# Block A's attention values as one 128-column stationary operand in a two-layer hybrid attention encoder

## The chip, the cores and the metric

One core of one Trainium2 chip runs the whole program in one launch. The metric is the device time of that launch in microseconds (us), the median over the runs shown; lower is better. The kernel before takes 1463.04 us (three runs, 1462.65 to 1463.38).

## The reference, cut to what matters

Two layers, each with three kinds of attention (A, B, C) on a sequence of 1024 and a width of 1024. The change is in the weighted sum of the values of A, the dilated attention of four heads of 64 features:

```python
DILATED_PATTERNS = ((128, 1), (512, 4), (2048, 16))
def dilated_attention(q, k, v, slopes):
    for window, dil in DILATED_PATTERNS:
        ...
        p = jnp.exp(s - m)
        den = jnp.sum(p, axis=-1, keepdims=True)
        o = jnp.einsum('bndhij,bnjdhe->bnidhe', (p / den).astype(v.dtype), vw)
        lse = (m + jnp.log(den))[..., 0]
        ...
    w = jax.nn.softmax(jnp.stack(lses, axis=0), axis=0)
    out = jnp.sum(w[..., None] * jnp.stack(outs, axis=0), axis=0)

    # in each layer
    ya = dilated_attention(qa, ka, va, slopes).reshape(B, S, A_WIDTH) * jax.nn.silu(ag)
    yb = dense_attention(qb, kb, vb) * jax.nn.silu(bg)
    yc = dense_attention(qc, kc, vc) * jax.nn.silu(cg)
    y = jnp.concatenate([ya, yb, yc], axis=-1)
    x = x + y @ w_out[l]
```

## The kernel before

Float32 products are made on TensorE from pairs: each operand is split into a high part (rounded to the type that TensorE takes in one pass) and a low part (the rest), and high x high, high x low and low x high are added up in PSUM. Values lie in scratch memory as 128 columns per head: 64 high, 64 low (`v_evac`), so that a tile of values can be loaded with both parts side by side.

A layer first makes the projections and the gates, and then runs the attention of 16 heads in an order that is planned by hand: `put(slot, step, priority)` files every step of every head under a slot of a common counter, and `slot` (L1219) emits the steps of one slot by priority. ScalarE (`A`) executes them in that order; on the other engines (`T` TensorE, `V` VectorE, `G` GpSimd) and in SyncE's queue of DMAs the scheduler of the language orders what has been emitted, by its own estimate of when operands are ready and by the order of emission. B's six heads come first, then A's four (slots `base_a + 4` to `base_a + 36` and some), then C's six; the scores of C's first head are made while A's last heads are worked on. Between A's steps stand partial output projections, `f_load`, `f_mm` and `f_add` (L1093 to L1124), of features that are already there. `f_load` fetches a piece of the output weights and a strip of x, has GpSimd split the weights, and is filed `FL` slots ahead of its products (L1190).

A head of A goes through these steps:
- `a_s` (L897 to L913): scores of the window pattern and of the "class" pattern (the two dilated ones, by residue of the position), bias and maximum by VectorE; `a_exp` (L920, L922): exponentials by ScalarE.
- The statistics chain, `a_x1` to `a_x5` (L926 to L986): small VectorE steps on columns of maxima and sums (L929, L944 to L951, L962 to L969, L983, L986), with two products by TensorE (L937, L977) that move values between partitions, and one exponential (L956). Out come the weights of the two patterns.
- `a_norm_w` (L992) and `a_norm_c` (L996): GpSimd multiplies the probabilities by those weights, eight tiles each.
- `a_t` (L1009, L1014, L1015, L1019, L1020): TensorE transposes them, and `split_pt` (L782, L783) splits them into high (`ph`) and low (`pl`) on ScalarE and VectorE.
- `a_v` (L1029 to L1068): the products with the values, in three passes with 64 stationary columns each: `w[:, LO]` with `ph`, `w[:, LO]` with `pl`, `w[:, HI]` with `ph` (L1038 to L1040 for the class, L1051 to L1053 for the window). All three add to the same 64 PSUM partitions.
- `a_end` (L1077): ScalarE copies the class result into `y` (L1085), VectorE adds the window result to it (L1088). After the second head of a pair GpSimd multiplies by the gate (`fin_gate`, L820), and ScalarE and GpSimd split the product (`fin_split`, L836, L837).

The heads of B and C already use 128 stationary columns and two passes (`tv_v`, L801 and L802), with the halves added in `tv_end` (L839 to L854).

PSUM tiles of 512 columns for transposes and for accumulators come from the same four buffers. `H` (L67) is a pool of six SBUF buffers of 512 columns that holds, among others, the split output weights of `f_load` and the copies `t0` and `t1` of `tv_end`.

Of the kernel before, what the change touches and what calls it, by code (L numbers as in the profile page):

```python
# [11 lines left out]
AF = mybir.ActivationFunctionType  # L12
ALU = mybir.AluOpType
AX = mybir.AxisListType

P = 128
# [21 lines left out]
def hybrid_encoder(  # L38
# [8 lines left out]
    V, G, A, T = nc.vector, nc.gpsimd, nc.scalar, nc.tensor  # L47

    cp = ctx.enter_context(tc.tile_pool(name="consts", bufs=1))
    sp = ctx.enter_context(tc.tile_pool(name="work", bufs=1))  # L50
# [6 lines left out]
    def nm(s):  # L57
        uid[0] += 1
        return f"{s}_{uid[0]}"
# [5 lines left out]
        return sp.tile(list(shape), dt, tag="QB", name=nm("qb"), bufs=8)  # L65

    def H(dt=F32, shape=(P, 512)):  # L67
        return sp.tile(list(shape), dt, tag="H", name=nm("h"), bufs=6)

    def WR(dt=F32, shape=(P, 512)):  # L70
        return sp.tile(list(shape), dt, tag="Wr", name=nm("wr"), bufs=3)
# [203 lines left out]
    def layer(l, xh, xl, ss, g, bg_x):  # L275
# [14 lines left out]
        for k in range(8):  # L290
# [12 lines left out]
            for m, half in order:  # L303
                w = slice(m * P, m * P + P)
                o = bk[m][half]
                s = slice(half * 512, half * 512 + 512)
# [90 lines left out]
        for k in range(8):  # L397
            w = ws.next(3)
# [4 lines left out]
            if k == SK:  # L403
                lat_stats()
                r, r2, fq, fkv = lat_factors()
# [30 lines left out]
        for c in range(NCH):  # L436
            s = slice(c * P, (c + 1) * P)
            pq = PS()
            for half in range(2):
                o = pq[:, half * 512:half * 512 + 288]  # L440
                w = slice(half * 288, half * 288 + 288)
# [6 lines left out]
        for c in range(NCH):  # L448
            s = slice(c * P, (c + 1) * P)
# [262 lines left out]
        LO, HI = slice(0, 64), slice(64, 128)  # L712
# [65 lines left out]
        accs, PTs = {}, {}  # L778
# [250 lines left out]
        def a_v(h, i):  # L1029
            ph, pl = PTs.pop(("a", h, i))  # L1030
            if i < 4:
                if i % 2 == 0:
                    accs["a", h, "c"] = PA()
                o = accs["a", h, "c"][LO, (i % 2) * 256:(i % 2) * 256 + 256]
                for kb in range(2):
                    w = Vcl[h][:, 2 * i + kb, :]
                    s = slice(kb * 256, kb * 256 + 256)
                    T.matmul(o, w[:, LO], ph[:, s], start=(kb == 0), stop=False)  # L1038
                    T.matmul(o, w[:, LO], pl[:, s], start=False, stop=False)
                    T.matmul(o, w[:, HI], ph[:, s], start=False, stop=(kb == 1))  # L1040
                if i % 2 == 1:
                    a_end(h, "c", i // 2)
                return
            if i == 4:
                accs["a", h, 0] = PA()
            if i == 5:
                accs["a", h, 1] = PA()

            def mm(half, q0, w, rows, cols, start=False, stop=False):
                o = accs["a", h, half][LO, q0 * P:q0 * P + (cols.stop - cols.start)]  # L1050
                T.matmul(o, w[rows, LO], ph[rows, cols], start=start, stop=False, skip_group_check=True)  # L1051
                T.matmul(o, w[rows, LO], pl[rows, cols], start=False, stop=False, skip_group_check=True)
                T.matmul(o, w[rows, HI], ph[rows, cols], start=False, stop=stop, skip_group_check=True)  # L1053

            full = slice(0, P)
            if i == 4:
                mm(0, 0, Vs[h][:, 1, :], full, slice(0, 256), start=True)
                mm(0, 1, Vs[h][:, 2, :], full, slice(256, 512))
            elif i == 5:
                mm(0, 2, Vs[h][:, 3, :], full, slice(0, 256))  # L1060
                mm(0, 3, Vs[h][:, 4, :], full, slice(256, 384))
                mm(1, 0, Vs[h][:, 4, :], full, slice(384, 512), start=True)
            elif i == 6:
                mm(1, 0, Vs[h][:, 5, :], full, slice(0, 256))
                mm(1, 1, Vs[h][:, 6, :], full, slice(256, 512))
            else:
                mm(0, 0, Vs[h][:, 0, :], LO, slice(256, 384), stop=True)
                mm(1, 2, Vs[h][:, 7, :], full, slice(0, 256))  # L1068
                mm(1, 3, Vs[h][:, 8, :], LO, slice(384, 512), stop=True)
                a_end(h, 0, 0)  # L1070
                a_end(h, 1, 1)
                for n in range(4):
                    Pa.pop((h, n))
# [3 lines left out]
        def a_end(h, what, half):  # L1077
            acc = accs.pop(("a", h, what))
            fc, par = feat(("a", h))
            if fc not in pairs:  # L1080
                gate_load(fc)
            rows = slice(64 * par, 64 * par + 64)
            y = pairs[fc][0]
            if what == "c":
                A.activation(y[rows, half * 512:half * 512 + 512], acc[LO], AF.Copy)  # L1085
            else:
                yv = y.rearrange("p (r s i) -> p s r i", r=4, s=2)[rows, half]
                V.tensor_tensor(yv, acc[LO].rearrange("p (i r) -> p r i", r=4), yv, ALU.add)  # L1088


        Fw, Fx, Fp = {}, {}, {}
# [43 lines left out]
        start = {hd: 16 * i + (8 * AH + AT0 if hd[0] == "c" else 0) for i, hd in enumerate(heads)}  # L1135
# [6 lines left out]
        for i, hd in enumerate(heads):  # L1142
            for c in range(NCH):
                s = start[hd] + 2 * c - LAG_D
# [36 lines left out]
        for h in range(AH):  # L1181
# [4 lines left out]
            if h % 2:  # L1186
                for half in range(2):
                    put(base_a + AT0 + 8 * h + FA[0] + half, lambda h=h, half=half: fin_gate(h // 2, half), 6)
                    put(base_a + AT0 + 8 * h + FA[1] + half, lambda h=h, half=half: fin_split(h // 2, half), 6)
        F0, FN, FP, FL = -10, 5, 6.5, 8  # L1190
        for i, m in enumerate(EARLY):
            s = base_a + F0 + FN * i
            put(s - FL, lambda m=m: f_load(m), 9)
# [5 lines left out]
        for i, hd in enumerate(heads):  # L1199
            kind, h = hd  # L1200
# [259 lines left out]
```

## Time and profile before

| | before |
|---|---|
| median of 3 runs | 1463.04 us |
| profiled execution | 1461.05 us |
| its span | 1459.1 us |
| instructions | 23134 |
| TensorE busy | 1443.1 us (99%) |
| VectorE busy | 1094.5 us (75%) |
| ScalarE busy | 899.4 us (62%) |
| GpSimd busy | 574.3 us (39%) |
| granted TensorE clock | 1.00 |

The span runs from the first to the last instruction of the profiled execution; the 1.95 us more of its own time lie around it. PE is TensorE's products, PEld its weight loads, DVE VectorE, ACT ScalarE, POOL GpSimd, SPq SyncE's DMA queue. Products are pipelined, so the busy time of one in the trace is longer than its share of the engine; the share is read from start to start.

### The profile page before, as it was taken

The numbers are of one execution on the slowest core, as the hardware profiler recorded it, in microseconds if no ns is written. First come the engines' busy times: TensorE is split into PE (matmuls) and PEld (weight loads), VectorE is DVE, ScalarE is ACT, GpSimd is POOL, SyncE is SP. The second block draws the span as 40 slices with busy tenths as digits, with TensorE's granted clock in tenths as the row PEclk, the third lists the DMA queues.
The fourth block names the chain that finished last, engine by engine and source line by source line (L and its number), as shares of the span: only waits on it lengthen the run. The fifth ranks groups of instructions, "written<-read, shape, count | busy, mean of one in ns | idle before, by whom it ended". The sixth has DMA issues, their size and how long they took to land.

```text
span 1459.1 us, 23134 instructions
## 1 busy us (share of the span) xinstructions
PE 1443.1 (99%) x7912; PEld 1227.4 (84%) x7912; DVE 1094.5 (75%) x1997; ACT 899.4 (62%) x1678; POOL 574.3 (39%) x516
## 2 busy tenths in 40 slices
PE   9999999999999999999999999999999999999999
PEld 7998888888888888888889988888888888888887
DVE  7759767488888789994736597574888787899942
ACT  6473234488888769993425723343888886799820
POOL 6204431135455565550322054211454554754500
PEclk9999999999999999999999999999999999999999
DMA  6261136610287821102622611465103688121143
GB/s 223 80 245 59 52 107 207 207 44 30 51 202 204 243 84 51 44 26 75 212 81 90 238 40 47 166 198 156 59 30 76 172 242 235 31 59 30 44 148 121
DMA packets 118134, 171.81 MB, mean 118 GB/s; under 512 B 11520, under 2 KB 73088, under 8 KB 118016
## 3 DMA queue, kind: packets, MB, share of 16 engines
q1 hardware_dynamic: 118016, 170.32, 38.2%
q8 instruction: 63, 1.03, 0.3%
q14 instruction: 55, 0.45, 0.1%
HBM read 109.47 MB, written 60.82 MB: 117 GB/s over the span
## 4 chain that ended last, share of the span: by engine, by line
PE 90%; DVE 4%; ACT 3%; DMA 1%; issue 1%; SPq 0%; POOL 0%; ACTq 0%; DVEq 0%
PE S L760 15%; PE T L789 11%; PE acc L802 6%; PE acc L801 6%; PE T L669 4%; PE T L667 4%; PE T L668 4%; PE S L1262 3%; PE S L1260 3%; PE S L1261 3%; PE S L221 2%; PE S L222 2%; PE S L223 2%; PE T L705 1%; PE T L221 1%
## 5 line engine op out<-in xcount | busy, mean ns | idle before, releaser
L783 DVE TENSOR_TENSOR wl<-T,wh 128x512 fp32r<-128x512 f32 x440 | 297.0, 685 | 69.2 <-ACT wh L782 67.2
L782 ACT ACTIVATE wh<-T 128x512 fp32r<-128x512 f32 x440 | 261.2, 596 | 115.7 <-PE T L789 77.4
L776 POOL TENSOR_SCALAR u<-u,rec 128x1024 f32<-128x1024 f32 x192 | 216.5, 1128 | 277.4 <-DVE rec L775 176.7
L760 PE MATMUL S<-u,u 96*128 96x512 f32 (+1 forms) x960 | 268.7, 409 | 0.5 <-ACT u L769 0.3
L762 DVE TENSOR_REDUCE nmax<-S 128x1 f32<-128x1024 f32 x192 | 233.7, 1217 | 23.7 <-PE S L760 23.2
L789 PEld LDWEIGHTS T<-ident,u 128*128 128x128 f32 x1536 | 190.8, 140 | 49.0 <-DVE wl L783 0.4
L789 PE MATMUL T<-ident,u 128*128 128x128 f32 x1536 | 230.0, 272 | 0.0
L769 ACT ACTIVATE u<-S,nmax 128x1024 f32<-128x1024 f32 x192 | 213.2, 1111 | 0.3
L150 POOL TENSOR_TENSOR wl<-wr,wh 128x512 fp32r<-128x512 f32 (+2 forms) x48 | 75.1, 1567 | 320.4 <-ACT wh L146 314.9
L760 PEld LDWEIGHTS S<-u,u 96*128 96x128 f32 (+1 forms) x960 | 166.7, 189 | 27.9 <-ACT u L769 1.4
L146 ACT ACTIVATE wh<-wr 128x512 fp32r<-128x512 f32 (+2 forms) x96 | 56.9, 596 | 157.6 <-PE S L222 97.3
L667 PE MATMUL T<-u,wh 128*128 128x512 f32 x256 | 102.1, 399 | 0.0
L669 PE MATMUL T<-u,wl 128*128 128x512 f32 x256 | 100.1, 391 | 0.0
L668 PE MATMUL T<-u,wh 128*128 128x512 f32 x256 | 99.9, 390 | 0.0
L801 PE MATMUL acc<-wh,u 128*128 128x512 f32 x192 | 84.5, 440 | 0.0
L801 PE MATMUL acc<-wh,qb 128*128 128x512 f32 x192 | 82.8, 431 | 0.0
L802 PE MATMUL acc<-wl,u 128*128 128x512 f32 x192 | 76.1, 396 | 2.5 <-DVE wl L783 2.5
L802 PE MATMUL acc<-wl,qb 128*128 128x512 f32 x192 | 76.1, 397 | 0.1
L150 DVE TENSOR_TENSOR wl<-wr,wh 128x512 fp32r<-128x512 f32 (+2 forms) x48 | 41.5, 865 | 44.2 <-ACT wh L146 44.2
L1260 PE MATMUL S<-u,qb 128*128 128x512 f32 x186 | 74.1, 398 | 0.0
L1262 PE MATMUL S<-u,qb 128*128 128x512 f32 x186 | 73.2, 394 | 0.0
L1261 PE MATMUL S<-u,qb 128*128 128x512 f32 x186 | 72.9, 392 | 0.0
(294 smaller groups left out, 3342.0 us busy)
## 6 DMA issues: line engine op xcount, KB each, us to landing
u<-qk_c SPq DMA_DIRECT2D x40, 256.0 KB, 4.1
wr<-in_w_g_dram SPq DMA_DIRECT2D x32, 256.0 KB, 2.6
gates<-h SPq DMA_DIRECT2D x32, 256.0 KB, 2.3
qk_c<-u SPq DMA_DIRECT2D x16, 512.0 KB, 4.0
u<-gates SPq DMA_DIRECT2D x16, 512.0 KB, 3.6
qb<-qk_a SPq DMA_DIRECT2D x32, 256.0 KB, 5.9
vb<-u SPq DMA_DIRECT2D x16, 384.0 KB, 3.3
u<-vb SPq DMA_DIRECT2D x12, 512.0 KB, 4.8
```

The source lines that it names most:

```text
L667: T.matmul(ps[half], wh[:, w], xh[k][:, s], start=(k == 0), stop=False)
L668: T.matmul(ps[half], wh[:, w], xl[k][:, s], start=False, stop=False)
L669: T.matmul(ps[half], wl[:, w], xh[k][:, s], start=False, stop=(k == 7))
L760: T.matmul(ps[:, w], q[:, s], k[:, w], start=(i == 0), stop=(i == len(terms) - 1))
L762: V.tensor_reduce(nmax, ps, op=ALU.max, axis=AX.X, negate=True)
L769: A.activation(p, ps, AF.Exp, bias=nmax, accum_out=den)
L776: G.tensor_scalar(p, p, rec, 1.0, ALU.mult, ALU.mult)
L782: A.activation(ph, ps, AF.Copy)
L783: V.tensor_tensor(pl, ps, f32(ph), ALU.subtract)
L789: T.transpose(ps[:, i * P:(i + 1) * P], Pt[hd, 4 * half + i][0][:, j * P:(j + 1) * P], ident)
L801: T.matmul(acc, w, ph, start=(j == 0), stop=False)
L802: T.matmul(acc, w, pl, start=False, stop=(j == 7))
```

## The change

The values' tile is used whole, with its 128 columns, as stationary operand, for two passes (`ph` and `pl`), and the result takes 128 PSUM partitions: the products with the high part of the values in the lower 64, those with the low part in the upper 64. `a_end` adds the two halves: for the class, two ScalarE copies (upper half to a new `H` tile `t1`, lower half to `y`) and a GpSimd addition; for the window, a ScalarE copy of the upper half to `t1`, a VectorE addition of the lower half to `t1`, and a GpSimd addition to `y`. The low x low product, which the three passes leave out, is now in the sum. `H` gets a seventh buffer, and `f_load` is filed five slots ahead of its products and not eight.

```diff
@@ -65,7 +65,7 @@
     def H(dt=F32, shape=(P, 512)):
-        return sp.tile(list(shape), dt, tag="H", name=nm("h"), bufs=6)
+        return sp.tile(list(shape), dt, tag="H", name=nm("h"), bufs=7)
@@ -1031,13 +1031,12 @@
-                o = accs["a", h, "c"][LO, (i % 2) * 256:(i % 2) * 256 + 256]
+                o = accs["a", h, "c"][:, (i % 2) * 256:(i % 2) * 256 + 256]
                 for kb in range(2):
                     w = Vcl[h][:, 2 * i + kb, :]
                     s = slice(kb * 256, kb * 256 + 256)
-                    T.matmul(o, w[:, LO], ph[:, s], start=(kb == 0), stop=False)
-                    T.matmul(o, w[:, LO], pl[:, s], start=False, stop=False)
-                    T.matmul(o, w[:, HI], ph[:, s], start=False, stop=(kb == 1))
+                    T.matmul(o, w, ph[:, s], start=(kb == 0), stop=False)
+                    T.matmul(o, w, pl[:, s], start=False, stop=(kb == 1))
@@ -1047,10 +1046,9 @@
             def mm(half, q0, w, rows, cols, start=False, stop=False):
-                o = accs["a", h, half][LO, q0 * P:q0 * P + (cols.stop - cols.start)]
-                T.matmul(o, w[rows, LO], ph[rows, cols], start=start, stop=False, skip_group_check=True)
-                T.matmul(o, w[rows, LO], pl[rows, cols], start=False, stop=False, skip_group_check=True)
-                T.matmul(o, w[rows, HI], ph[rows, cols], start=False, stop=stop, skip_group_check=True)
+                o = accs["a", h, half][:, q0 * P:q0 * P + (cols.stop - cols.start)]
+                T.matmul(o, w[rows], ph[rows, cols], start=start, stop=False, skip_group_check=True)
+                T.matmul(o, w[rows], pl[rows, cols], start=False, stop=stop, skip_group_check=True)
@@ -1081,11 +1079,19 @@
             y = pairs[fc][0]
+            t1 = H()
             if what == "c":
-                A.activation(y[rows, half * 512:half * 512 + 512], acc[LO], AF.Copy)
+                out = y[rows, half * 512:half * 512 + 512]
+                A.activation(t1[rows], acc[HI], AF.Copy)
+                A.activation(out, acc[LO], AF.Copy)
+                G.tensor_tensor(out, out, t1[rows], ALU.add)
             else:
                 yv = y.rearrange("p (r s i) -> p s r i", r=4, s=2)[rows, half]
-                V.tensor_tensor(yv, acc[LO].rearrange("p (i r) -> p r i", r=4), yv, ALU.add)
+                tv = t1[rows].rearrange("p (r i) -> p r i", r=4)
+                lo, hi = (acc[part].rearrange("p (i r) -> p r i", r=4) for part in (LO, HI))
+                A.activation(tv, hi, AF.Copy)
+                V.tensor_tensor(tv, lo, tv, ALU.add)
+                G.tensor_tensor(yv, yv, tv, ALU.add)
@@ -1187,7 +1193,7 @@
-        F0, FN, FP, FL = -10, 5, 6.5, 8
+        F0, FN, FP, FL = -10, 5, 6.5, 5
```

## Rows read from the trace of the kernel before

**Rows 1.** The page's first part: busy time and share of the span by engine.

```profile
PE 1443.1 (99%) x7912; PEld 1227.4 (84%) x7912; DVE 1094.5 (75%) x1997; ACT 899.4 (62%) x1678; POOL 574.3 (39%) x516
```

**Rows 2.** Stretches: length, busy time by engine (instructions), granted clock, DMA share, GB/s.

```profile
474.70:545.00 70.30, 67.44 (x492) 59.37 (x490) 58.36 (x155) 48.83 (x125) 41.07 (x65) 1.00 0.57 164
1198.00:1268.00 70.00, 67.15 (x491) 59.13 (x489) 58.08 (x155) 48.53 (x125) 40.77 (x65) 1.00 0.53 155
560.00:580.00 20.00, 20.00 (x119) 16.81 (x118) 19.30 (x33) 17.61 (x33) 9.59 (x9) 1.00 0.30 80
```

**Rows 3.** Instructions of the third pass: count, min/median/max ns, first and last start, forms.

```profile
L1040 PE MATMUL acc<-wh,qb x64: 274/280/283, 475.0 to 1256.7; 128*64 128x256 f32 x64
L1053 PE MATMUL acc<-wh,qb x80: 217/277/282, 485.7 to 1263.7; 128*64 128x256 f32 x48, 128*64 128x128 f32 x16, 64*64 64x128 f32 x16
```

**Rows 4.** Timeline of TensorE, layer 1: start us, us, engine, line, instruction.

```profile
500.81 0.28 PE L897 MATMUL S<-qb,u 128*128 128x256 f32 x1
500.93 0.28 PE L898 MATMUL S<-qb,u 128*128 128x256 f32 x1
...
501.76 0.27 PE L1014 MATMUL T<-ident,u 128*128 128x128 f32 x1
501.87 0.27 PE L1015 MATMUL T<-ident,u 128*128 128x128 f32 x1
...
502.60 0.28 PE L1040 MATMUL acc<-wh,qb 128*64 128x256 f32 x1
502.72 0.28 PE L1038 MATMUL acc<-wh,qb 128*64 128x256 f32 x1
...
508.31 0.22 PE L1052 MATMUL acc<-wl,qb 128*64 128x128 f32 x1
508.37 0.22 PE L1053 MATMUL acc<-wh,qb 128*64 128x128 f32 x1
...
509.73 0.41 PE L937 MATMUL T<-z,order 128*128 128x64 f32 x2 [0.50 <-DVE wl L1026]
...
510.21 0.28 PE L1053 MATMUL acc<-wh,qb 128*64 128x256 f32 x1
...
514.58 0.28 PE L1040 MATMUL acc<-wh,qb 128*64 128x256 f32 x1
...
517.95 0.38 PE L977 MATMUL T<-z,order 128*128 128x32 f32 x2 [1.73 <-DVE z L969]
```

**Rows 5.** What ends a head now (min/median/max ns), and a GpSimd addition of 64x512.

```profile
L1085 ACT ACTIVATE u<-acc x16: 583/592/592, 479.7 to 1257.0; 64x512 f32<-64x512 f32 x16
...
L1088 DVE TENSOR_TENSOR u<-acc,u x16: 673/674/685, 495.7 to 1264.8; 64x512 f32<-64x512 f32 x16
...
472.01 1.30 POOL L854 TENSOR_TENSOR u<-h,h 64x512 f32<-64x512 f32 x1
```

**Rows 6.** Chain of waits, layer 1, where it runs through ScalarE: start us, us, what.

```profile
479.77 0.48 ACT u L1085
```

**Rows 7.** Timeline of VectorE at the last statistics chain of layer 1.

```profile
513.99 1.11 DVE L962 TENSOR_TENSOR t<-st,e 128x16 f32<-128x16 f32 x1
515.13 1.46 DVE L963 TENSOR_TENSOR rc<-t 128x8 f32<-128x8 f32 x1
...
517.40 0.18 DVE L966 TENSOR_TENSOR sc<-e,rc 128x16 f32<-128x16 f32 x1
```

**Rows 8.** Timeline of GpSimd in layer 1.

```profile
476.25 1.01 POOL L1104 TENSOR_TENSOR h<-wr,h 128x384 fp32r<-128x384 f32 x1
...
513.50 3.07 POOL L820 TENSOR_TENSOR u<-u,u 128x512 f32<-128x512 f32 x2 [5.45 <-issue]
```

**Rows 9.** Two steps of the statistics chain over the whole span: count, min/median/max ns.

```profile
L962 DVE TENSOR_TENSOR t<-st,e x8: 163/586/1109, 461.4 to 1237.3; 128x16 f32<-128x16 f32 x8
...
L963 DVE TENSOR_TENSOR rc<-t x8: 149/166/1461, 462.9 to 1238.4; 128x8 f32<-128x8 f32 x8
```

**Rows 10.** Chain of waits, layer 1: the last partial output projection, a first product.

```profile
498.87 0.23 PE T L1116
```

## The prediction

> **What bounds the kernel now.** The first view is the page's list of engines: TensorE is busy for 99% of the span, VectorE for 75%, ScalarE for 62%, GpSimd for 39% [rows 1]. That is an average over stages, so the second view cuts out the stretches in which A's four heads of each layer are transposed and multiplied with their values. They are 70.3 and 70.0 us long and alike: TensorE 67.4 and 67.2 us busy, VectorE 58, ScalarE 49, GpSimd 41 [rows 2]. TensorE is the fullest engine, but not alone: the gaps of these stretches are short waits for others. In the stage of C behind it TensorE shows 20.00 us in 20 and VectorE 19.30 [rows 2], so time that is saved in A's stretch is not needed by anybody later, and a delay of it is not made up there either. The clock is granted in full, 1.00 [rows 2], which is the 2.4 GHz level, before and, as the engine stays busy, after.
>
> Third, the instructions one by one. The third pass stands 64 times on L1040 and 80 times on L1053, 18 per head and 144 in all: 112 of 256 columns, 16 of 128, and 16 of 128 with 64 rows [rows 3]. The timeline tells what each holds of the engine, from start to start: 0.12 us with 256 columns and 64 stationary ones, and the same 0.12 us with 256 columns and 128 stationary ones, in the scores of A [rows 4]. With 128 columns it is 0.06 us for 64 stationary ones, and 0.11 us for 128, in the transposes [rows 4].
>
> Fourth, the chain around the one clear wait of TensorE in this stage: between L937 and L977 of the last head lie 8.2 us, and at the end TensorE stands for 1.73 us until VectorE has the factors [rows 4].
>
> **The passes.** Per head 14 passes of 256 columns go, 14 x 0.12 = 1.68 us; two passes remain with 128 stationary columns at the old price [rows 4]. The two products of 128 columns go from 3 x 0.06 = 0.18 to 2 x 0.11 = 0.22 us, so they lose 0.08 per head. For the two with 64 rows no row shows 128 stationary columns: each is bounded by that loss of 0.04 and by a gain of one pass, 0.06; I take the middle, 0.02 for both. The sum is 1.62 us per head, 6.5 a layer, 13.0 in all.
>
> **Where that is not gained.** Inside the 8.2 us of the last head's chain nine third passes lie, from 510.21 to 514.58 [rows 4]: seven of 256 columns and two of 64 rows, 0.9 us. TensorE waits at the end of that chain already, so without them it only waits longer. 0.9 us per layer is lost, between nothing (other products of C are brought forward into the gap) and 0.9.
>
> **ScalarE.** The class result takes two copies in place of one, the window result one in place of none: four more per head at 0.59 us [rows 5], 9.5 us a layer, on 49 busy of 70 [rows 2]. That is about 90% of the shorter stretch, and ScalarE keeps the order it is given: whatever is behind a copy waits for the product that fills the accumulator, the high parts (L782) that TensorE needs next among them. Most of it lies beside TensorE's work. One place doesn't: around 480 us the chain of waits runs through ScalarE, and the class copy is a link of 0.48 us in it [rows 6]. A second copy there costs another 0.5 us per layer; the bounds are nothing and four copies per layer, 2.4.
>
> **VectorE.** It has as many instructions as before: two additions per head from PSUM at 0.67 us [rows 5]. But each now waits for a copy, and behind it in VectorE's queue are the steps L962 to L966 of another head's chain [rows 7]. In the last head that is on the path: 0.59 us later.
>
> **GpSimd.** Four additions of 64x512 per head, taken as L854's 1.30 us [rows 5]: 20.8 us a layer on 41.1 [rows 2]. In the shorter stretch that is about 95%. The more costly thing is what they do to VectorE. L962 and L963 take 0.16 and 0.15 us undisturbed [rows 9]; in the last chain they take 1.11 and 1.46, and end at 515.10 and 516.59, as GpSimd's two gate products (513.50 to 516.57) end [rows 7, 8]. So 2.26 us of the chain were lost to 3.07 us of GpSimd. Now two window additions, 2.6 us, come ahead of these gate products, and the gate products move back onto L966 and L969, of which L966 now takes 0.18 us [rows 7]. The cost is between 0 and 2.6 us per layer. I take 1.1, below the middle because VectorE has other work from PSUM to do between these steps. With the copy, 1.7 us per layer.
>
> The Trainium skill says the same as these rows, and more (SBUF — State Buffer, "Who interferes with whom"): a VectorE instruction with two SBUF inputs and a GpSimd instruction that reads SBUF use a shared read interface that the first one holds to its end, while the other blocks altogether. L962 and L963 agree with it at 1.11 and 1.46 us. It speaks against this change, since every addition that is moved to GpSimd can hold a chain step; what that would make of the time is the last rival below.
>
> **Accumulators, H and f_load.** Accumulators are read 0.5 to 0.6 us later (the copy), and they share four buffers with the transposes. No row shows what a later release costs, so 0 to 0.6 us per head; I take 0, as the only long wait of TensorE here is one for VectorE's factors [rows 4]. `t1` needs an `H` buffer from the copy to GpSimd's addition, and there is one more. `f_load` moves three slots later, some 6 us: two DMAs on SyncE's queue, which go behind A's loads that were filed after them, and two GpSimd steps, for six strips a layer. I cost it at nothing: the last split ends at 477.26, over 20 us ahead of its last products at 498.87 [rows 8, 10]. Were that cover gone, the products would wait for their weights, by at most those 6 us a layer.
>
> **The sum.** Per layer -6.5 + 0.9 + 0.5 + 1.7 = -3.4 us, twice -6.8. The profiled execution took 1461.05 us (span 1459.1, 1.95 around it), which would become 1454.3. The median of the runs is 2.0 us above it; the forecast for the median is 1463.04 - 6.8 = **1456.2 us**, with 1453 to 1459.5 for this case alone.
>
> **Rivals.** *All of it comes through.* If the scheduler fills the chain's gap with products of C, and the copies and additions fall into idle time of their engines, the full 13.0 us is gained: 1450.0. For it speaks that GpSimd stands idle for 5.45 us just ahead of the place [rows 8], against it that TensorE already waits there. *GpSimd late.* If the two class additions, 2.6 us, run ahead of the last head's normalisations (L992, L996), behind the gate products [rows 8] on the same engine, its transposes wait for them: 2 x 2.6 back, 1461.4, no change that could be told. The same result stands if the passes didn't get cheaper in number, that is if two passes with 128 columns cost as much as three; the scores at 0.12 us [rows 4] speak against that, and I give it next to nothing. *Slower: GpSimd holds VectorE's chain.* If additions hold chain steps as the gate products do, each us of GpSimd costs 2.26 / 3.07 = 0.74 us, and a head's 5.2 us cost 3.8. Three heads a layer end beside a following chain: 11.5 us a layer if all of it strikes, of which 1.1 is in the sum. From one third on, the gain is used up; at two thirds it is (7.7 - 1.1) x 2 = 13.2 us, 1469.4. For it speak [rows 7] and the median of L962, 0.59 us against 0.16 at best; against it L963, whose median of 0.17 us says that most of its eight executions were undisturbed [rows 9].
>
> **How the numbers follow.** Chances: the forecast 0.46, all of it 0.28, GpSimd late 0.15, slower 0.11. A measurement of this kernel can tell about 0.2%, 2.9 us, from no change: faster is below 1460.1, slower above 1466.0. Faster gets 0.44 + 0.28 + 0.03 = 0.75, the same 0.16 (the rest of the forecast, most of GpSimd late, a weak form of the last rival), slower 0.09. The range goes from 1449.5 (all of it, with the 64-row passes at their better bound) to 1464.0 (GpSimd late, with its bounds); it leaves out most of the last rival and the edges of the first.
>
> **What would show it.** In the trace after: L1040 and L1053's third passes gone, 256-column passes still 0.12 us apart, 128-column ones 0.11; A's stretches some 3.4 us shorter each, stages outside them unchanged; the wait before L977 in the last head longer than 1.73 us; L962 to L966 held by GpSimd's additions; GpSimd over 60 us busy in the stretch. The forecast is wrong if the stretches shrink by 6 us, or not at all, or if stages without A change.

## The result: slower by 1.26%, and the profile after

The changed kernel takes 1480.29 us (median of four runs, 1479.56 to 1480.55), the kernel before beside it on the same chip 1462.85: a ratio of 1.0126 [1.0113, 1.0139], 17.4 us slower. Forecast were 1456.2 us, in a range from 1449.5 to 1464.0. The profiled execution took 1479.56 us, its span is 1477.8.

The page's first part, after; it answers to [rows 1]:

```profile
PE 1442.8 (98%) x7768; PEld 1222.9 (83%) x7768; DVE 1105.6 (75%) x1997; ACT 917.3 (62%) x1710; POOL 613.9 (42%) x548
```

The 144 third passes are gone (7912 - 7768 products), the 32 copies and 32 additions are there (1678 to 1710, 516 to 548). The next view is that of [rows 2]: A's first stretch, and then slices of it (length; busy us and instructions of PE, PEld, DVE, ACT, POOL; granted clock; DMA share; GB/s).

```profile
474.70:545.00 70.30, 58.53 (x375) 50.31 (x373) 57.23 (x137) 49.15 (x123) 53.35 (x75) 0.95 0.59 171
...
515.00:520.00 5.00, 3.31 (x22) 2.65 (x21) 4.97 (x9) 2.73 (x5) 4.55 (x4) 1.00 0.98 334
520.00:525.00 5.00, 0.00 (x0) 0.00 (x0) 5.00 (x4) 0.00 (x0) 5.00 (x9) 0.66 0.61 163
525.00:530.00 5.00, 4.84 (x30) 4.87 (x30) 2.13 (x5) 2.00 (x4) 3.71 (x9) 0.66 0.00 0
```

In the same 70.3 us TensorE gets through 375 products instead of 492, and from 520 to 525 through none, while VectorE and GpSimd are busy without a break. VectorE does four instructions in those 5 us. TensorE's waits from 474 to 560 say for what it stood; the two longest in total (total us, times, longest):

```profile
PE T L977 <- DVE z L969: 8.4, 2, 6.9
PE T L1009 <- POOL u L1087: 0.9, 2, 0.7
```

In before, L977 waited once in this window, 1.73 us [rows 4]; now the last head waits 6.86 and the third head, which did not wait at all, 1.56. The chain of waits of the last head, one line per piece (start us, us, what), is the centre of the result:

```profile
511.21 0.41 PE T L937 x2
...
513.75 0.60 ACT h L1092
514.38 1.29 DVE h L1093 x2
515.69 0.84 DVE t L962
516.53 0.60 DVE wl L783
517.13 1.05 DVE rc L963
518.19 0.60 DVE wl L783
518.90 1.09 DVE nmax L762
519.99 1.13 DVE sc L966
521.12 0.60 DVE wl L783
521.72 3.30 DVE z L969
525.03 0.14 issue
525.16 0.60 PE T L977 x2
```

From L937 to L977 it is 13.95 us, 8.2 before. L969 alone is 3.30 us long in the chain. GpSimd's timeline (start us, us, line, instruction, idle time ahead of it) shows what runs beside it:

```profile
515.21 1.28 POOL L1094 TENSOR_TENSOR u<-u,h 64x512 f32<-64x512 f32 x1 [2.91 <-DVE h L1093]
516.58 1.59 POOL L820 TENSOR_TENSOR u<-u,u 128x512 f32<-128x512 f32 x1
518.24 1.26 POOL L1094 TENSOR_TENSOR u<-u,h 64x512 f32<-64x512 f32 x1
519.58 1.51 POOL L820 TENSOR_TENSOR u<-u,u 128x512 f32<-128x512 f32 x1
521.05 1.26 POOL L1087 TENSOR_TENSOR u<-u,h 64x512 f32<-64x512 f32 x1
522.29 3.54 POOL L992 TENSOR_SCALAR u<-u,sc 128x192 f32<-128x192 f32 x8
```

L962, L963 and L966 end as L1094, L820 and L820 end. L969 starts beside a class addition (VectorE's timeline has it from 521.65 on, for 3.37 us) and gets through only after six of the eight normalisations of L992 behind it. In before it ran 0.12 us ahead of that burst and took 0.19 us, as VectorE's and GpSimd's timelines of before show:

```profile
517.62 0.19 DVE L969 TENSOR_TENSOR z<-sc,order 128x32 f32<-128x32 f32 x1
...
517.74 3.57 POOL L992 TENSOR_SCALAR u<-u,sc 128x192 f32<-128x192 f32 x8 [1.17 <-issue]
```

The steps that were held read two tiles in SBUF; L783, which reads one operand from PSUM, takes its usual 0.60 us in the middle of the same burst. The Trainium skill (SBUF — State Buffer, "Who interferes with whom") says that a VectorE instruction with two SBUF inputs contends with a GpSimd instruction that reads SBUF, and that one with at most one SBUF input, outside VectorE's two-port modes, does not. The rows agree, with L969's 3.30 us on the one side and L783's 0.60 on the other.

Last, TensorE's timeline behind the wait (as [rows 4]):

```profile
525.94 0.41 PE L1039 MATMUL acc<-wl,qb 128*128 128x256 f32 x1
526.15 0.41 PE L1038 MATMUL acc<-wh,qb 128*128 128x256 f32 x1
...
529.01 0.28 PE L1050 MATMUL acc<-wh,qb 128*128 128x256 f32 x1
529.13 0.28 PE L1051 MATMUL acc<-wl,qb 128*128 128x256 f32 x1
...
529.98 0.27 PE L1051 MATMUL acc<-wl,qb 128*128 128x128 f32 x1
530.09 0.27 PE L1050 MATMUL acc<-wh,qb 128*128 128x128 f32 x1
```

The passes cost what was forecast, 0.12 us with 256 columns and 0.11 with 128. But for 3 us after the wait they are 0.21 us apart: the granted clock is 0.66 on average from 520 to 530, where it was 1.00; in slices of 2 us it is 0.50 from 524 to 528, so there TensorE ran at 1.2 GHz.

### The profile page after: what moved, and what is told of

It reads as the page before. It is cut to its first block, busy times and chain, and to the rows that moved or that the text cites. A ratio compares the mean times of both kernels' runs of the same rounds, so it can differ in the third digit from the quotient of the medians.

```text
span 1477.8 us, 22933 instructions
## 1 busy us (share of the span) xinstructions
PE 1442.8 (98%) x7768; PEld 1222.9 (83%) x7768; DVE 1105.6 (75%) x1997; ACT 917.3 (62%) x1710; POOL 613.9 (42%) x548
## 4 chain that ended last, share of the span: by engine, by line
PE 85%; DVE 7%; ACT 3%; DMA 2%; issue 2%; POOL 1%; SPq 0%; ACTq 0%; POOLq 0%; DVEq 0%
PE S L760 15%; PE T L789 11%; PE acc L802 6%; PE acc L801 6%; PE T L667 4%; PE T L669 4%; PE T L668 4%; PE S L1266 3%; PE S L1268 3%; PE S L1267 3%; PE S L221 2%; PE S L222 2%; PE S L223 2%; PE T L705 1%; DVE wl L783 1%
## 5 line engine op out<-in xcount | busy, mean ns | idle before, releaser
L783 DVE TENSOR_TENSOR wl<-T,wh 128x512 fp32r<-128x512 f32 x440 | 297.0, 685 | 72.7 <-ACT wh L782 70.6
L776 POOL TENSOR_SCALAR u<-u,rec 128x1024 f32<-128x1024 f32 x192 | 215.9, 1125 | 270.6 <-DVE rec L775 154.3
L762 DVE TENSOR_REDUCE nmax<-S 128x1 f32<-128x1024 f32 x192 | 233.7, 1217 | 26.8 <-PE S L760 26.4
L789 PEld LDWEIGHTS T<-ident,u 128*128 128x128 f32 x1536 | 191.2, 140 | 51.7 <-POOL u L776 1.9
L789 PE MATMUL T<-ident,u 128*128 128x128 f32 x1536 | 230.6, 272 | 1.5 <-POOL u L776 1.5
L802 PE MATMUL acc<-wl,u 128*128 128x512 f32 x192 | 76.1, 396 | 3.4 <-DVE wl L783 3.4
L802 PE MATMUL acc<-wl,qb 128*128 128x512 f32 x192 | 76.1, 396 | 0.1
```

The source lines that it names most:

```text
L762: V.tensor_reduce(nmax, ps, op=ALU.max, axis=AX.X, negate=True)
L776: G.tensor_scalar(p, p, rec, 1.0, ALU.mult, ALU.mult)
L783: V.tensor_tensor(pl, ps, f32(ph), ALU.subtract)
L789: T.transpose(ps[:, i * P:(i + 1) * P], Pt[hd, 4 * half + i][0][:, j * P:(j + 1) * P], ident)
L802: T.matmul(acc, w, pl, start=False, stop=(j == 7))
```

## The experiments

Theory: GpSimd's additions hold VectorE's chain by reading SBUF. Rivals: ScalarE's copies come too late; GpSimd is simply occupied, and what waits for its output is late; the seventh `H` buffer and the later `f_load` cost something. Differences below are each taken from the kernel before beside the run (1461.4 to 1462.85 us); by their intervals each is good to 1 to 2 us, and a step between two of them to 2 or 3.

### One part at a time

**e1, the passes alone.** `a_end` as before.

```diff
-                A.activation(t1[rows], acc[HI], AF.Copy)
-                A.activation(out, acc[LO], AF.Copy)
-                G.tensor_tensor(out, out, t1[rows], ALU.add)
+                A.activation(y[rows, half * 512:half * 512 + 512], acc[LO], AF.Copy)
...
-                A.activation(tv, hi, AF.Copy)
-                V.tensor_tensor(tv, lo, tv, ALU.add)
-                G.tensor_tensor(yv, yv, tv, ALU.add)
+                V.tensor_tensor(yv, acc[LO].rearrange("p (i r) -> p r i", r=4), yv, ALU.add)
```

> The two passes of 128 stationary columns, H and f_load as in the changed kernel, but a head ends as before: only the lower 64 partitions are read, no extra copy and no GpSimd addition. The low part of the values is left out of the result. Theory (GpSimd's additions hold VectorE's statistics chain): the passes are a gain by themselves, 1463 - 6 to 13 = 1450 to 1457 us, and the wait before the last L977 is back at about 2 us. Rival Q (passes with 128 stationary columns, or the 64-row ones, cost more than they save): stays near 1480. Rival R (f_load's later place): stays above 1463 too.

1456.41 us, 0.9956 [0.9941, 0.9971]: the passes alone gain 5.8 us. L977's last wait is 1.86 us. So the passes are a gain, and the loss comes from what adds the halves, the copies included.

**e2, the additions alone** (with their copies), with three passes as before and copies scaled by zero.

```diff
-                A.activation(t1[rows], acc[HI], AF.Copy)
+                A.activation(t1[rows], acc[LO], AF.Copy, scale=0.0)
```

> The three passes of before, with the changed kernel's H and f_load and with its way to end a head: the copy to t1 has scale 0, so the additions add zeros. Theory: the additions alone make the kernel slower by what the changed kernel lost and its passes gained, 1463 + 17 + 6 to 13 = 1486 to 1493 us, with L962 to L969 of the last chain held by GpSimd for 4 to 6 us. Rival Q: near 1463.

1474.75 us, 1.0083 [1.0066, 1.01]: 12.5 us slower, half of what was expected. L977 hardly waits; TensorE stands elsewhere, as its timeline shows:

```profile
517.02 0.38 PE L977 MATMUL T<-z,order 128*128 128x32 f32 x2 [0.43 <-DVE z L969]
...
525.10 0.33 PE L1009 MATMUL T<-ident,u 128*128 128x128 f32 x1 [2.29 <-POOL u L996]
```

TensorE's transposes wait 3.6 us in all for normalisations, which two class additions (at 522.93 and 525.02) hold up: the rival "GpSimd late". So the same additions can cost by holding VectorE's chain or by standing ahead of GpSimd's own normalisations, depending on where they fall.

**e4, `H` and `f_load` alone**, on the kernel before.

```diff
-        return sp.tile(list(shape), dt, tag="H", name=nm("h"), bufs=6)
+        return sp.tile(list(shape), dt, tag="H", name=nm("h"), bufs=7)
...
-        F0, FN, FP, FL = -10, 5, 6.5, 8
+        F0, FN, FP, FL = -10, 5, 6.5, 5
```

> The kernel before with the change's seventh H buffer and later f_load alone. Theory: nothing, 1463 within 0.2%, since the split weights are there over 15 us ahead of their products. Rival (f_load's GpSimd steps and DMAs now fall on the chain or on A's loads): 1466 or more, which would be part of what the additions-only kernel lost.

1463.09 us, 1.0008 [0.9999, 1.0017]: no difference that can be told. This rival falls.

**e3, both halves added by VectorE from PSUM**, no GpSimd, no further copy.

```diff
-                A.activation(t1[rows], acc[HI], AF.Copy)
-                G.tensor_tensor(out, out, t1[rows], ALU.add)
+                V.tensor_tensor(out, acc[HI], out, ALU.add)
...
+                for part in (LO, HI):
+                    V.tensor_tensor(yv, acc[part].rearrange("p (i r) -> p r i", r=4), yv, ALU.add)
```

> The changed kernel, both halves added by VectorE straight from PSUM (four more VectorE instructions of 0.67 us per head, no extra ScalarE copy, no GpSimd addition). Theory: GpSimd no longer holds the chain, so it is faster than 1480 by over 8 us; VectorE has 10.8 us more per layer on 58 of 70, which gives back some: 1455 to 1470. Rival Q: stays at 1480 or, with VectorE's work on top, above it.

1465.51 us, 1.0025 [1.0016, 1.0035]: 14 us of the 17 are gone, yet it doesn't reach the kernel before. L969 is back at 0.18 us. The copies are gone here too, so this run does not tell them from GpSimd's additions. VectorE's 16 further additions a layer make other VectorE work late instead: L1014 waits 1.3 us in all for the splits of L783, and the last L977 2.02.

**e5, three of the 16 additions of a layer moved to VectorE** (window of the second head, one class addition of the third).

```diff
+            if (h, what) == (2, "c") and half == 0:
+                ...
+                V.tensor_tensor(out, acc[HI], out, ALU.add)
+            if h == 1 and what != "c":
+                ...
```

> The changed kernel with 3 of the 16 additions of a layer taken off GpSimd and made by VectorE from PSUM: the two window additions of the second head and the first class addition of the third head, which are those that run beside the last statistics chain. Theory: the wait before the last L977 falls from 6.9 us to 1 to 3 us, the clock stays granted, and the kernel gains 4 to 7 us per layer: 1466 to 1472. Rival (GpSimd's or ScalarE's load in general): a gain in proportion, 3/16 of the loss, 3 us: 1477.

1472.77 us, 1.0068 [1.0053, 1.0083]: with three of 16 additions moved, 6.9 of 17.4 us are gone. L977's last wait falls from 6.86 to 2.23, the third head's stays at 1.57. Where an addition stands counts more than how many there are.

**e7, L969 on GpSimd**, in its own order ahead of L992.

```diff
-            V.tensor_tensor(z[:, 0:32].rearrange("p (r c) -> p r c", r=4),
+            G.tensor_tensor(z[:, 0:32].rearrange("p (r c) -> p r c", r=4),
```

> The changed kernel with one small instruction moved: the product of L969 (128x32, two SBUF inputs) runs on GpSimd, ahead of its normalisations, instead of on VectorE. Theory: in the last chain that product no longer waits behind GpSimd's class addition and six normalisations, the wait before the last L977 falls from 6.9 to 3 to 4.5 us and the clock stays up: 1480 - 2 x (3 to 4) = 1472 to 1474. Rival (the chain is late for another reason, GpSimd's load as such): no more than 1 us gained, 1479 or above.

1476.07 us, 1.0101 [1.0085, 1.0116]: 3.4 of the 17.4 us are gone, half of what was expected. GpSimd's timeline:

```profile
522.64 1.25 POOL L1087 TENSOR_TENSOR u<-u,h 64x512 f32<-64x512 f32 x1
523.86 0.23 POOL L969 TENSOR_TENSOR z<-sc,order 128x32 f32<-128x32 f32 x1
```

The step itself takes 0.23 us there, so the 3.30 were waiting; L977's wait falls to 4.23, not further, since the step now stands in line behind L1087 and the steps ahead of it are still held.

### Occupied, or reading?

**e12, copies but no GpSimd additions.** The low half is copied and left out of the sum.

```diff
-                G.tensor_tensor(out, out, t1[rows], ALU.add)
...
-                V.tensor_tensor(tv, lo, tv, ALU.add)
-                G.tensor_tensor(yv, yv, tv, ALU.add)
+                V.tensor_tensor(yv, lo, yv, ALU.add)
```

> The changed kernel without GpSimd's additions: ScalarE's extra copies stay, VectorE adds the lower half to y as before, and the low part of the values is left out. Theory: the copies cost little, 1456 (the passes alone) + 0 to 3 = 1456 to 1459, so that GpSimd's additions make up nearly all of what the changed kernel loses. Rival R (ScalarE's copies, which VectorE and the release of accumulators wait for): 1465 or more.

1464.55 us, 1.0018 [1.0009, 1.0027]: 8.5 us more than e1, where 0 to 3 were expected. Here VectorE's window addition does not wait for a copy, and yet the copies cost nearly what rival R says.

**e6, three memsets of GpSimd in place of each addition**, otherwise e12: GpSimd is occupied for somewhat longer, but reads nothing.

```diff
+                for _ in range(3):
+                    G.memset(t1[rows], 0.0)
```

> As the kernel with the copies only, but where the changed kernel has a GpSimd addition there are three GpSimd memsets of the copy, which write SBUF and read nothing; the low part of the values is left out. Theory (a GpSimd instruction that reads SBUF holds VectorE's steps with two SBUF inputs): L962 to L969 of the last chain stay at 0.2 us beside a memset, and the kernel is within 4 us of the one with the copies only. Rival (GpSimd's load alone, its normalisations coming late): slower by what the memsets take, in proportion to GpSimd's busy time.

1470.44 us, 1.0061 [1.0047, 1.0075]: 5.9 us more than e12, above the 4 that were expected, so the rival has a part in it: GpSimd's time costs by itself. Of e6's last chain, GpSimd's timeline and under it VectorE's:

```profile
513.23 2.86 POOL L1098 MEMSET h<- 64x512 f32 x6 [0.66 <-ACT h L1095]
516.17 1.54 POOL L820 TENSOR_TENSOR u<-u,u 128x512 f32<-128x512 f32 x1
...
518.12 1.52 POOL L820 TENSOR_TENSOR u<-u,u 128x512 f32<-128x512 f32 x1
```

```profile
514.46 0.18 DVE L962 TENSOR_TENSOR t<-st,e 128x16 f32<-128x16 f32 x1
...
515.15 0.15 DVE L963 TENSOR_TENSOR rc<-t 128x8 f32<-128x8 f32 x1
...
517.34 0.41 DVE L966 TENSOR_TENSOR sc<-e,rc 128x16 f32<-128x16 f32 x1
...
518.27 1.43 DVE L969 TENSOR_TENSOR z<-sc,order 128x32 f32<-128x32 f32 x1
```

L962 and L963 run beside six memsets at their undisturbed 0.18 and 0.15 us; L966 meets the end of a gate product and takes 0.41, and L969 falls on the next one, which reads, and takes 1.43. It is the reading that holds VectorE. The Trainium skill (SBUF — State Buffer, "Who interferes with whom") says that a GpSimd instruction which only writes doesn't contend; these rows agree.

**e14 and e15, the class copy and the window copy, each alone** on e1.

```diff
+                A.activation(t1[rows], acc[HI], AF.Copy)      e14, class
+                A.activation(tv, hi, AF.Copy)                 e15, window
```

> The passes with the extra ScalarE copy of the class result alone (two per head), nothing added from it; the low part of the values is left out. If the copies' 8 us come from the class copies, which lie in ScalarE's own link of the chain of waits: 1461 to 1464; if they come from the window copies: near 1456.5.

> The passes with the extra ScalarE copy of the window result alone (two per head), nothing added from it; the low part of the values is left out. If the copies' 8 us come from the window copies, which lie beside the last statistics chain, with a longer wait before L977 and a clock that falls after it: 1461 to 1464; if from the class copies: near 1456.5.

e14: 1456.07 us, 0.996 [0.9946, 0.9973], as e1: by themselves the class copies are free. e15: 1458.69, 0.9981 [0.9971, 0.999], 2.6 us more than e1, between what its text gives for the one case and for the other. Both together (e12) cost 8.5. The clock has a part in that, and e15 shows it best, because its two layers are alike up to there (53.41 us from L977 of A's first head to the last one, in both): TensorE's last L977 of each layer, and the 5 us slice behind each.

```profile
518.50 0.38 PE L977 MATMUL T<-z,order 128*128 128x32 f32 x2 [2.69 <-DVE z L969]
1239.44 0.38 PE L977 MATMUL T<-z,order 128*128 128x32 f32 x2 [2.69 <-DVE z L969]
```

```profile
520.00:525.00 5.00, 4.83 (x37) 4.30 (x36) 2.91 (x6) 5.00 (x11) 5.00 (x12) 1.00 0.09 19
...
1240.00:1245.00 5.00, 5.00 (x33) 4.93 (x32) 2.25 (x6) 3.79 (x8) 5.00 (x13) 0.66 0.03 9
```

The same wait of 2.69 us, but the clock fell behind it in layer 2 only, and there A's stretch (first L977 to A's last product) is 74.06 us instead of 73.01: this fall costs 1.05 us. In e12 it fell in both layers. That explains some 2 us of e12's 8.5, and the longer wait (2.69 against 1.86) under 2. The rest stays open; most of it lies behind the last L977, where A's last product comes 22.63 us later in e12 and 20.65 in e15's second layer, both with the lower clock.

### The additions out of A's stretch

**e8**: one 128-row copy and one 128-row window addition per half, no halves added in A; the folding, the gate and the split are filed in the stage of C.

```diff
+                A.activation(y[:, half * 512:half * 512 + 512], acc, AF.Copy)
...
+                V.tensor_tensor(yv, acc.rearrange("p (i r) -> p r i", r=4), yv, ALU.add)
...
+        def a_fold(fc, half):
+            A.activation(t1[LO], ye[HI, w], AF.Copy)
+            A.activation(t1[HI], yo[LO, w], AF.Copy)
+            G.tensor_tensor(ye[LO, w], ye[LO, w], t1[LO], ALU.add)
+            G.tensor_tensor(ye[HI, w], yo[HI, w], t1[HI], ALU.add)
```

> The two passes of 128 columns, with all 128 rows of the result kept: the class copy and the window addition work on 128 rows at the old count of instructions, and the halves are folded (two ScalarE copies, two GpSimd additions per half and pair of heads) together with the gate and the split in C's stage, where no VectorE instruction has two SBUF inputs. H and f_load as before. Theory: as fast as the passes alone (1456) or faster, since the gate products no longer hold the chain either: 1449 to 1457. Rival Q (128 rows and columns cost by themselves): 1463 or more.

1473.31 us, 1.0085 [1.0069, 1.01], far above the 1449 to 1457 of the theory. It is not rival Q, though: A's stretches are 5.8 us shorter each, and the stage of C gives more than that back: L789 waits 4.1 us in layer 1 for GpSimd's L776, behind the folds.

**e9**, the kernel before with A's gate and split filed there.

```diff
-                    put(base_a + AT0 + 8 * h + FA[0] + half, lambda h=h, half=half: fin_gate(h // 2, half), 6)
+                    put(s + 5 + half, lambda h=h, half=half: fin_gate(h // 2, half), 6)
```

> The kernel before, with the gate and split of A's features moved to C's stage and nothing else. Theory: L962 and L963 of the last chain take 0.2 us each instead of 1.1 and 1.5, the wait before the last L977 goes from 1.7 to near 0, and 1 to 2 us per layer are gained: 1459 to 1461. Rival (the chain waits for something else): 1463.

1466.76 us, 1.0033 [1.0019, 1.0047], 4.7 us slower, for reasons that were not followed. This one told nothing of the chain, since the gate products did not move:

```profile
514.27 3.08 POOL L820 TENSOR_TENSOR u<-u,u 128x512 f32<-128x512 f32 x2 [5.47 <-issue]
```

They still run beside L962 and L963, though filed later: only ScalarE executes in the filed order. What is to run later on GpSimd must be given an operand that comes later.

**e10 and e13**: the halves are brought to the right partitions by DMA, one 128-row addition per half adds them, and the gate product waits for a late load of the gate. e13 files these steps between others' work instead of further back.

```diff
+            nc.scalar.dma_start(yt[fc][LO, w], ye[HI, w])
+            nc.scalar.dma_start(yt[fc][HI, w], yo[LO, w])
...
+            nc.scalar.dma_start(ye[HI, w], yo[HI, w])
+            G.tensor_tensor(ye[:, w], ye[:, w], yt[fc][:, w], ALU.add)
...
+            nc.scalar.dma_start(pairs[fc][1][:, w], gates[fc, :, w])
```

> The two passes with all 128 rows kept as in the kernel that folded in C's stage, but the halves are brought together by three small DMAs per half and pair of heads, issued from ScalarE's queue in C's stage, and added by one GpSimd instruction of 128x512 per half; gate and split are spread over that stage, one GpSimd instruction at a time. Theory: A's stretches are shorter by 5 to 6 us each, as in that kernel, and C's stage no longer gives it back, since GpSimd's normalisations are held by no more than 1.6 us at a time: 1450 to 1454, faster than both kernels. Rival (any GpSimd work in C's stage costs what it takes): 1456 to 1462.

> As the kernel with the folds spread over C's stage, with folds, gates and splits of A moved to slots in which C's own pairs have no gate and split on GpSimd (pair 0 from slot 42 to 60, pair 1 from 75 to 93). Theory: A's stretches keep their 5.8 us, and C's stage gives back 1 to 3 us per layer instead of 8: 1452 to 1457, faster than before. Rival (GpSimd work in C's stage costs wherever it is): 1462 to 1465 again.

e10: 1464.12 us, 1.0017 [1.0008, 1.0026]. e13: 1462.15, 1.0003 [0.9994, 1.0011], no difference from before. Again 5.8 us per stretch are gained, and the stage of C gives them back. For e10 that is more than its rival had allowed; e13 comes out where its rival put it, but e16 below speaks against the reason that the rival gives.

**e16**, e13 with SyncE issuing those DMAs instead of ScalarE; **e17**, the same with wider distances.

```diff
-            nc.scalar.dma_start(yt[fc][LO, w], ye[HI, w])
+            nc.sync.dma_start(yt[fc][LO, w], ye[HI, w])
```

> The kernel that folds the two halves in the stage of C by DMA and one GpSimd addition per half (e13), with its DMAs issued by SyncE in place of ScalarE. A's stretches are to stay 5.8 us shorter each. If ScalarE's DMA issues and their waits are what the stage of C gives back, C returns at most 2 us a layer and the time is 1453 to 1457; if GpSimd's additions, gate products and the later split are, it stays at 1461 to 1464. If SyncE's queue stalls behind the folds (it also carries the loads of weights for the output projection), slower than 1464.

> As e16, with more slots between the DMAs, the additions, the gates and the splits (5 and 6 in place of 3 and 4). If the waits of C come from work that stands too close to what it waits for, this is 1 to 3 us faster than e16; if from the amount of work on GpSimd and VectorE, the same within 1 us.

e16: **1451.16 us, 0.9929 [0.9915, 0.9942]**, 10.2 us faster than before and faster than e13 by 10.5, and below the 1453 to 1457 expected. e17: 1451.43, 0.9933 [0.9921, 0.9946], the same. TensorE's waits from 535 to 620 in e13:

```profile
PE acc L802 <- DVE wl L783: 2.3, 4, 1.0
PE T L789 <- POOL u L776: 0.5, 1, 0.5
```

In e16 that view is empty. GpSimd's additions and gates are as many in both, so the engine that issues makes the difference. How it does so is only in part seen. Each issue takes a place in ScalarE's queue, but ScalarE's work has the same order in both kernels. What differs is the order that the scheduler gave VectorE and GpSimd. Ahead of e13's longest wait, a product L802 at 552.47, VectorE's timeline has:

```profile
550.59 1.23 DVE L762 TENSOR_REDUCE nmax<-S 128x1 f32<-128x1024 f32 x1 [1.07 <-PE S L760]
551.73 1.28 DVE L783 TENSOR_TENSOR wl<-T,wh 128x512 fp32r<-128x512 f32 x2
```

ScalarE had the high parts for these two splits ready at 548.94 and 550.26, but a maximum (L762) stands ahead of them and waits for TensorE's scores. In e16 the two splits come first there. So the late splits of e13 come from VectorE's order; whether the time that ScalarE takes for the issues costs anything besides was not shown.

And VectorE's last chain in e16, where GpSimd's first instruction is L992 at 514.67:

```profile
511.49 0.17 DVE L962 TENSOR_TENSOR t<-st,e 128x16 f32<-128x16 f32 x1
...
512.37 0.16 DVE L963 TENSOR_TENSOR rc<-t 128x8 f32<-128x8 f32 x1
...
515.48 0.18 DVE L969 TENSOR_TENSOR z<-sc,order 128x32 f32<-128x32 f32 x1
```

L962 and L963 have no GpSimd instruction beside them; L969 runs among normalisations and is not held. e16 computes all that the changed kernel does, with two passes of 128 columns, and beats both kernels. How much of its gain comes from the gate products' new place was not tried on the kernel before, since e9 did not move them.

## Why the prediction was wrong

The steps add up like this, each against its own kernel before:

| step | from | us |
|---|---|---|
| passes | e1 - before | -5.8 |
| four more ScalarE copies per head | e12 - e1 | +8.5 |
| GpSimd occupied | e6 - e12 | +5.9 |
| GpSimd reading | after - e6 | +8.9 |
| sum | after - before | +17.4 |

Each step is measured on top of the ones above it, and in another order it could cost otherwise (e2: copies and additions without the passes cost 12.5). The last step changes more than the reading: VectorE's window additions now wait for a copy, and the gate products for the additions. By place, from the starts in TensorE's timeline, in us after L977 of A's first head in layer 1:

| | L937, last head | L977, last head | A's last product | first L977 of layer 2 |
|---|---|---|---|---|
| before | 44.98 | 53.20 | 75.61 | 723.31 |
| e1 | 43.49 | 52.44 | 72.03 | 720.27 |
| e12 | 44.21 | 54.00 | 76.63 | 724.57 |
| e6 | 44.12 | 53.99 | 78.05 | 728.33 |
| after | 46.05 | 60.00 | 83.35 | 732.70 |
| e16 | 42.35 | 50.53 | 69.78 | 718.78 |

The forecast was -3.4 us a layer, the result is +8.7 by the medians. Of these 12.1 us the passes missed 2.7 (-2.9 in place of -5.6), ScalarE's copies 3.1 (+4.2 in place of 0.5 and 0.6), and GpSimd's additions 6.3 (+7.4 in place of 1.1).

**The passes (-6.5, of which 0.9 lost: -5.6 a layer): right in e16, too much by 2 in e1.** Of a layer's 72 third passes 31 start ahead of the last head's L937, nine between it and L977, and 32 behind, so that the forecast by place is 2.8, nothing and 2.9 us. e16 gains 2.6, nothing (8.18 us from L937 to L977, 8.22 before) and 3.2: 5.8. e1 gains 1.5 and 2.8, and its last chain is 0.7 us longer: 3.6, or 2.9 by the medians. The 64-row passes with 128 stationary columns were priced too well: two of them take 0.36 us in e16 from start to start (522.07 to 522.43), where three took 0.32 in before (525.88 to 526.20), so a head gains 1.52 us and not 1.62. What holds e1 up ahead of the last chain was not tried; it differs from e16 in A's gate products, which stand beside the chain, and in `H` and `f_load`.

**ScalarE (+0.5 a layer).** The class copy, the one I put on the path, cost nothing (e14). The window copy, which I charged 0.59, cost 1.3 a layer (e15), and all four together 4.2, more than both terms with their upper bounds (2.4 and 0.59); where the rest arises is open, as said at e15. The link that I priced, VectorE's addition waiting for the copy, is in the chain of waits (L1092, L1093), but costs 0.2 us at most: from L937 to L962 it is 4.48 us, 4.26 before, as VectorE is busy with a split until the copy ends.

**GpSimd holds VectorE's chain (+1.1 a layer, at most 2.6): this is the step that failed.** Its mechanism is what happened, its size was not. I counted two window additions ahead of the gate products, and held L966 and L969 for a part of that. In the trace additions and gate products alternate, a class addition follows, and then L992, nearly without a gap: 10.6 us of reading instructions (515.21 to 525.83). By VectorE's timeline L962, L963, L966 and L969 take 0.84 + 1.13 + 1.21 + 3.37 = 6.55 us. In e12, which has the same order of VectorE's steps and no addition, they take 1.05 + 0.99 + 0.16 + 0.19 = 2.39. The difference, 4.2 us a layer, is all that lies between the chains of the two (13.95 and 9.79 us). The bound of 2.6 us came from the added instructions alone, though a delayed step can fall into what was there already: L969 lost its place 0.12 us ahead of the normalisations.

Another 1.6 us of the chain (9.79 us in e12, 8.2 before) came without any addition. Three L783 and one L762, 2.9 us, stand between the chain's steps in e12 and in the changed kernel, where one L783 stood before: the scheduler gave VectorE another order, and the prediction has no term for that. The rival "GpSimd holds VectorE's chain" was right, at a chance of 0.11; its 1469.4 priced the holds of additions and left out the normalisations, this order and the clock.

**The clock ("granted in full before and, as the engine stays busy, after"): wrong.** The wait of 6.86 us was followed by products 0.21 us apart until 528.3, some 1.3 us per layer (twelve products from 525.58 to 528.29 took 2.7 us in place of eight at 0.12 and four at 0.11). A wait that grows can be paid for twice, by itself and behind itself.

**GpSimd late (a rival, +2.6 a layer).** It has a part: L1009 waits 0.9 us for L1087, the class additions ahead of the normalisations. With memsets, which hold nothing, GpSimd's added time cost 5.9 us (e6), 3 a layer; by the table it arises behind the last L977 and in C's stage, not in the chain. In e2 this rival was the larger part.

**Accumulators, `H` and `f_load` at nothing:** e4 bears it out for the last two. What a later release of the accumulators costs was not tried by itself and may be in the open rest of e12.

**Stages without A (unchanged):** not quite. Of the 9.4 us by which layer 1 is longer in the trace, 7.7 have arisen by A's last product and 1.7 come behind it. One wait of 0.8 us is seen there: L789 waits for GpSimd's L776, which stands behind the last head's additions and gate products.

## What to carry to other kernels

Before an addition goes to an idle GpSimd, look for short VectorE steps with two SBUF operands on the path beside it, and count everything GpSimd reads from there to its next idle time, not only what is added. If the sum can wait, move its parts to a stage where VectorE has no such chain, and try which engine issues the DMAs: from SyncE the same two passes gained 10 us instead of losing 17, with A's gate products moved as well, and from ScalarE nothing. Look at VectorE's order in the new trace before blaming a wait on the engine that was changed. To make GpSimd do something later, give it an operand that arrives later.

## What the runs showed of the hardware

- A held VectorE step can stay held over several GpSimd instructions that follow each other without a gap: in the changed kernel the last L969 stood through a class addition and six normalisations of 0.44 us, 3.37 us by VectorE's timeline, in both layers. It need not: in the third head of layer 1 of the same run it starts 0.09 us into the first normalisation and gets in behind that one, though the next follows at once, and in e16 it runs among normalisations in its 0.18 us. What decides this no run here shows. VectorE's and GpSimd's timelines at the third head:

```profile
503.74 0.37 DVE L969 TENSOR_TENSOR z<-sc,order 128x32 f32<-128x32 f32 x1
...
503.65 3.54 POOL L992 TENSOR_SCALAR u<-u,sc 128x192 f32<-128x192 f32 x8 [0.20 <-DVE sc L966]
```

- In e6 no step of VectorE's chain was held by a GpSimd memset of 64x512 (0.5 us each). In the changed kernel an addition of that size (1.28 us) and a gate product (1.5 us) held the steps with two SBUF operands that started in them, and L783, with an operand in PSUM, took its usual 0.6 us.
- TensorE's clock fell after a wait of 2.69 us in one layer of e15 and did not in the other; it cost 1.05 us. In e4 it fell in layer 1 alone, where L977 waits 1.72 us, about as in before: A's stretch there is 77.33 us long, 75.75 in layer 2. So a wait as long as that of the kernel before was followed by the lower clock once and, in before's two layers, was not.
